# Storing the last 64 rows of each partition in two transfers of 32 rows in place of four of 16

## The chip, the cores and the metric

One core of one Trainium2 chip. The metric is the device time of one execution in microseconds (us), the median over several runs. A profiled execution also has a span, which is about 1.8 us shorter than the time and is what the views of the profile count in. DVE, ACT, POOL and SP are the chip's VectorE, ScalarE, GpSimd and SyncE; SBUF is its on-chip memory, with 128 partitions.

## The reference

A softmax over the last axis of a 16 x 1024 x 512 tensor of float32: 16,384 rows of 512, or 128 rows of 2 KB for each of the 128 partitions. 33.55 MB are read and as much is written.

```python
def reference(x):
    x_max = np.max(x, axis=-1, keepdims=True)
    exp_x = np.exp(x - x_max)
    return (exp_x / np.sum(exp_x, axis=-1, keepdims=True)).astype(np.float32)
```

## The kernel before

Data is cut into chunks of so many rows per partition, at a place (row) of one large SBUF tile of 96 rows. Chunks 8 and 9 reuse the places of chunks 0 to 3. Work goes in groups of at most 8 rows: DVE takes the row maxima, ACT the exponentials with their sums, POOL (for the last three groups DVE) multiplies by the reciprocals. SP issues the loads, ACT the stores.

```python
CHUNKS = [
    (3, 0), (5, 3), (8, 8), (16, 16), (16, 32), (16, 48), (16, 64), (16, 80), (16, 0), (16, 16),
]
...
EARLY = 8                          # loads issued at the start
AFTER_STORE = {2: [8], 3: [9]}     # these two follow the stores of chunks 2 and 3
GROUP = 8
...
STORE_ROWS = {3: 8, 4: 8, 5: 8}    # chunks 3 to 5 are stored 8 rows at a time, others whole
ON_VECTOR = 3
...
    def scale(g):
        k, a, b, since = groups[g]
        ...                        # reciprocal, then POOL or DVE multiplies
        if since is not None:
            nc.scalar.dma_start(
                out=dst[k][:, since:b, :], in_=place[k][:, since:b, :]
            )
        if b == CHUNKS[k][0]:
            for later in AFTER_STORE.get(k, ()):
                load(later)
...
        for g, (k, a, _, _) in enumerate(groups):
            ...
            rowmax(g)
            exps(g)
            if waiting is not None:
                scale(waiting)     # one group behind
            waiting = g
```

The order in the last lines matters: a store stands in ACT's program after the exponentials of the next group, and ACT waits there until the multiplication is done.

Of the kernel before, what the change touches and what calls it, by code (L numbers as in the profile page):

```python
# [1 line left out]

# [4 lines left out]

F32 = mybir.dt.float32
EXP = mybir.ActivationFunctionType.Exp
AX = mybir.AxisListType.X  # L10


CHUNKS = [
    (3, 0), (5, 3), (8, 8), (16, 16), (16, 32), (16, 48), (16, 64), (16, 80), (16, 0), (16, 16),
]
SBUF_ROWS = 96

EARLY = 8
AFTER_STORE = {2: [8], 3: [9]}

GROUP = 8

FINISH_BEFORE = (1, 2, 3)

STORE_ROWS = {3: 8, 4: 8, 5: 8}

ON_VECTOR = 3

ON_ACT = ()

AT_HEAD = {mybir.EngineType.SP: 3}



def loads_at_the_head(nc):

    main, body = nc.main_func.blocks[0], nc.main_func.blocks[1]
    for engine, count in AT_HEAD.items():
        loads = [
            i  # L40
            for i in body.instructions
            if i.engine == engine and type(i).__name__ == "InstDMACopy"
        ][:count]
        barrier = next(
            n
            for n, i in enumerate(main.instructions)
            if i.engine == engine and type(i).__name__ == "InstDrain"
        )
        for load in loads:
            body.instructions.remove(load)  # L50
        main.instructions[barrier:barrier] = loads


def one_barrier_on_exit(nc):


    end = nc.main_func.blocks[2].instructions

    def of(engine, kind):
        return [i for i in end if i.engine == engine and type(i).__name__ == kind]  # L60

    for engine in (
        mybir.EngineType.Activation,
        mybir.EngineType.PE,
        mybir.EngineType.DVE,
        mybir.EngineType.SP,
    ):
        arrivals = [i for i in of(engine, "InstDrain") if i.has_update()]
        leaves = of(engine, "InstEventSemaphore")
        assert len(arrivals) == len(leaves) == 2  # L70
        end.remove(leaves[0])
        end.remove(arrivals[1])
    gather, release, gather_2, release_2 = of(mybir.EngineType.Pool, "InstEventSemaphore")
    end.remove(release)
    end.remove(gather_2)

@with_exitstack
def kernel(
    ctx: ExitStack,
    tc: tile.TileContext,  # L80
    x: bass.AP,
    out: bass.AP,
):
    nc = tc.nc
    nc.at_finalize(loads_at_the_head)
    nc.at_finalize(one_barrier_on_exit)
    P = nc.NUM_PARTITIONS

    x_flat = x.flatten_outer_dims()
    out_flat = out.flatten_outer_dims()  # L90
    n, d = x_flat.shape
    assert n == P * sum(R for R, _ in CHUNKS)


    src, dst, at = [], [], 0
    for R, _ in CHUNKS:
        for flat, views in ((x_flat, src), (out_flat, dst)):
            part = flat[at : at + P * R, :]
            views.append(part.rearrange("(p r) d -> p r d", r=R))
        at += P * R  # L100

    data = ctx.enter_context(tc.tile_pool(name="data", bufs=1))
    stats = ctx.enter_context(tc.tile_pool(name="stats", bufs=4))
    held = data.tile([P, SBUF_ROWS, d], F32, name="held")
    place = [held[:, s : s + R, :] for R, s in CHUNKS]


    groups = []
    for k, (R, _) in enumerate(CHUNKS):
        m = -(-R // GROUP)  # L110
        cuts = [R * i // m for i in range(m + 1)]
        since = 0
        for a, b in zip(cuts, cuts[1:]):
            ends = b == R or b - since >= STORE_ROWS.get(k, R)
            groups.append((k, a, b, since if ends else None))
            since = b if ends else since
    shift = [None] * len(groups)
    sums = [None] * len(groups)

    def load(k):  # L120
        queue = nc.scalar if k in ON_ACT else nc.sync
        queue.dma_start(out=place[k], in_=src[k])

    def rowmax(g):
        k, a, b, _ = groups[g]
        shift[g] = stats.tile([P, b - a], F32, name="shift", tag="shift")
        nc.vector.reduce_max(  # L127
            out=shift[g], in_=place[k][:, a:b, :], axis=AX, negate=True
        )

    def exps(g):
        k, a, b, _ = groups[g]
        sums[g] = stats.tile([P, b - a], F32, name="sums", tag="sums")
        for r in range(a, b):
            nc.scalar.activation(  # L135
                out=place[k][:, r, :],
                in_=place[k][:, r, :],
                func=EXP,
                bias=shift[g][:, r - a : r - a + 1],
                scale=1.0,  # L140
                accum_out=sums[g][:, r - a : r - a + 1],
            )

    def scale(g):
        k, a, b, since = groups[g]
        recip = stats.tile([P, b - a], F32, name="recip", tag="recip")
        nc.vector.reciprocal(out=recip, in_=sums[g])  # L147
        on_pool = g < len(groups) - ON_VECTOR
        if on_pool:
            nc.gpsimd.tensor_tensor(  # L150
                out=place[k][:, a:b, :],
                in0=place[k][:, a:b, :],
                in1=recip.unsqueeze(2).to_broadcast([P, b - a, d]),
                op=mybir.AluOpType.mult,
            )
        for r in () if on_pool else range(a, b):
            nc.vector.tensor_scalar_mul(  # L157
                out=place[k][:, r, :],
                in0=place[k][:, r, :],
                scalar1=recip[:, r - a : r - a + 1],  # L160
# [7 lines that stand above are left out]
                load(later)  # L168

    with tc.manual_schedule():  # L170
        for k in range(EARLY):
            load(k)
        waiting = None
        for g, (k, a, _, _) in enumerate(groups):
            if waiting is not None and a == 0 and k in FINISH_BEFORE:
                scale(waiting)
                waiting = None
# [3 lines that stand above are left out]
                scale(waiting)  # L181
            waiting = g
        scale(waiting)


# [1 line left out]
_INS = ['x']  # L187
_OUTS = [((16, 1024, 512), 'float32')]


# [23 lines left out]
```

## Time and profile before

| | before |
|---|---|
| time, median of 3 | 161.61 us |
| span of the profiled run | 159.63 us |
| DVE, ACT, POOL busy | 52%, 58%, 57% |
| DMA engines | 90% or more in 37 of 40 slices |
| the four 16-row stores issued | 96.32, 110.27, 120.35, 134.00 us |
| the same stores landed | 129.93, 139.58, 149.24, 158.90 us |

How to read it: an instruction that issues a DMA takes 0.34 us in the profile, while its bytes land 25 to 34 us later. A store's turn is the landing of the store ahead of it.

### The profile page before, as it was taken

How to read it: one execution, taken by the hardware profiler on the slowest of the kernel's cores; microseconds unless marked ns; L12 is line 12 of the kernel's file. 1: busy time of each engine (PE TensorE's matmuls, PEld its weight loads, DVE VectorE, ACT ScalarE, POOL GpSimd, SP SyncE). 2: the span in 40 equal slices, each digit the busy share in tenths (PEclk: the TensorE clock that was granted, in tenths of full speed). 3: DMA queues.
4: the chain of work that ended last, by engine and by line, in shares of the span. 5: the costliest groups of instructions: out<-in, count | busy, mean ns of one | idle time of the engine just before them, and what ended most of it. 6: DMA issues, size and time to landing. Idle time of an engine off the chain costs nothing.

```text
span 159.6 us, 442 instructions
## 1 busy us (share of the span) xinstructions
DVE 82.6 (52%) x58; ACT 92.9 (58%) x257; POOL 91.2 (57%) x18
## 2 busy tenths in 40 slices
DVE  0470903980966567393856768386479935000000
ACT  0719076039949796976979957993995760000000
POOL 0060912950899999999999999999930000000000
DMA  7999999999999999999999999989999999999994
GB/s 271 439 464 398 431 391 435 458 408 421 431 423 431 427 415 443 411 468 423 431 456 411 437 423 431 464 378 448 406 468 443 445 411 419 476 411 419 468 419 172
DMA packets 3315, 67.13 MB, mean 421 GB/s; under 512 B 368, under 2 KB 368, under 8 KB 624
## 3 DMA queue, kind: packets, MB, share of 16 engines
q1 hardware_dynamic: 1440, 33.56, 49.6%
q10 hardware_dynamic: 1872, 33.56, 49.0%
q14 instruction: 3, 0.02, 0.0%
HBM read 33.55 MB, written 33.55 MB: 420 GB/s over the span
## 4 chain that ended last, share of the span: by engine, by line
POOL 51%; issue 12%; ACT 11%; DVE 7%; DMA 3%; ACTq 0%; DVEq 0%; POOLq 0%
POOL held L150 51%; ACT held L135 11%; DVE held L157 4%; DMA held<-in_x_dram 3%; DVE shift L127 3%; ACTq L163 0%; DVE recip L147 0%; DVEq L209 0%; POOLq L150 0%; DVEq L147 0%; ACTq L135 0%
## 5 line engine op out<-in xcount | busy, mean ns | idle before, releaser
L135 ACT ACTIVATE held<-held,shift 128x512 f32<-128x512 f32 x128 | 90.4, 708 | 33.0 <-POOL held L150 29.9
L150 POOL TENSOR_TENSOR held<-held,recip 128x4096 f32<-128x4096 f32 (+2 forms) x14 | 91.0, 6529 | 25.8 <-DVE recip L147 25.8
L127 DVE TENSOR_REDUCE shift<-held 128x8 f32<-128x4096 f32 (+2 forms) x17 | 70.3, 4139 | 5.4 <-DMA held<-in_x_dram 5.4
L147 DVE RECIPROCAL recip<-sums 128x8 f32<-128x8 f32 (+2 forms) x17 | 3.4, 200 | 45.9 <-ACT held L135 45.9
L135 ACT ACTIVATION_READ_ACCUMULATOR held<-held,shift 128x1 f32 x128 | 24.0, 187 | 0.0
L157 DVE TENSOR_SCALAR held<-held,recip 128x512 f32<-128x512 f32 x24 | 10.0, 491 | 0.1
L135 ACT ACT_TABLE_LOAD x1 | 1.3, 1283 | 4.5 <-DMA held<-in_x_dram 4.5
L198 POOL MEMSET const-float32-0.0<- 128x1 f32 x1 | 0.1, 98 | 0.2 <-issue 0.2
L198 POOL MEMSET const-bfloat16-1.0<- 128x1 bf16 x1 | 0.1, 101 | 0.0
L198 POOL MEMSET const-uint8-127<- 128x1 uint8 x1 | 0.1, 101 | 0.0
L198 POOL MEMSET const-float32-1.0<- 128x1 f32 x1 | 0.1, 98 | 0.0
## 6 DMA issues: line engine op xcount, KB each, us to landing
held<-in_x_dram SPq DMA_DIRECT2D x7, 4096.0 KB, 39.1
out_dram<-held ACTq DMA_DIRECT2D x4, 4096.0 KB, 29.1
out_dram<-held ACTq DMA_DIRECT2D x7, 2048.0 KB, 37.9
held<-in_x_dram SPq DMA_DIRECT2D x1, 2048.0 KB, 11.5
held<-in_x_dram SPq DMA_DIRECT2D x1, 1280.0 KB, 7.1
out_dram<-held ACTq DMA_DIRECT2D x1, 1280.0 KB, 20.5
held<-in_x_dram SPq DMA_DIRECT2D x1, 768.0 KB, 4.4
out_dram<-held ACTq DMA_DIRECT2D x1, 768.0 KB, 15.8
```

What stands on the lines that cost most here:

```text
L127: nc.vector.reduce_max(out=shift[g], in_=place[k][:, a:b, :], axis=AX, negate=True)
L135: nc.scalar.activation(out=place[k][:, r, :], in_=place[k][:, r, :], func=EXP, bias=shift[g][:, r - a : r - a + 1], scale=1.0, accum_out=s ...
L147: nc.vector.reciprocal(out=recip, in_=sums[g])
L150: nc.gpsimd.tensor_tensor(out=place[k][:, a:b, :], in0=place[k][:, a:b, :], in1=recip.unsqueeze(2).to_broadcast([P, b - a, d]), op=mybir.A ...
L157: nc.vector.tensor_scalar_mul(out=place[k][:, r, :], in0=place[k][:, r, :], scalar1=recip[:, r - a : r - a + 1],)
L198: nc = _bacc.Bacc("TRN2", target_bir_lowering=False, num_devices=1)
```

## The change

Two chunks of 32 rows replace the last four of 16. Loads are still cut at 16 rows, so that compute need not wait for more and the early places can be filled as before. Only the stores grow: 32 rows of a partition are now contiguous in DRAM, and a chunk that is not in `STORE_ROWS` is stored whole. The intent is fewer and larger transfers at the end, where only stores are left.

```diff
-CHUNKS = [
-    (3, 0), (5, 3), (8, 8), (16, 16), (16, 32), (16, 48), (16, 64), (16, 80), (16, 0), (16, 16),
-]
+CHUNKS = [(3, 0), (5, 3), (8, 8), (16, 16), (16, 32), (16, 48), (32, 64), (32, 0)]
+
+LOAD_ROWS = 16
...
-    def load(k):
-        queue = nc.scalar if k in ON_ACT else nc.sync
-        queue.dma_start(out=place[k], in_=src[k])
+    loads = [
+        (k, a, min(a + LOAD_ROWS, R))
+        for k, (R, _) in enumerate(CHUNKS)
+        for a in range(0, R, LOAD_ROWS)
+    ]
+
+    def load(i):
+        k, a, b = loads[i]
+        nc.sync.dma_start(out=place[k][:, a:b, :], in_=src[k][:, a:b, :])
...
-        for k in range(EARLY):
-            load(k)
+        for i in range(EARLY):
+            load(i)
```

More of the change, by code (lines that the diff above doesn't have):

```diff
@@ L27 @@
 ON_VECTOR = 3
-ON_ACT = ()
 AT_HEAD = {mybir.EngineType.SP: 3}
```

## The prediction

> **What bounds the kernel now.** I read the page first, then the stretches, then the order of instructions near the end, then the DMA packets. The page is misleading in one place, and that place decides this case.
>
> ```profile
> DVE 82.6 (52%) x58; ACT 92.9 (58%) x257; POOL 91.2 (57%) x18
> DMA  7999999999999999999999999989999999999994
> DMA packets 3315, 67.13 MB, mean 421 GB/s; under 512 B 368, under 2 KB 368, under 8 KB 624
> POOL 51%; issue 12%; ACT 11%; DVE 7%; DMA 3%; ACTq 0%; DVEq 0%; POOLq 0%
> ```
>
> No compute engine is over 58% busy. The DMA row is at 90% or more in 37 of the 40 slices. The chain that ended last gives POOL 51%, which looks like a bound on POOL. But its shares add up to 84%: the chain follows instructions, and its last piece is a DVE multiplication that ends at 134.0 us of 159.6. The end of the kernel is not in it. What fills the last 25.6 us is seen when the span is cut into stretches (columns: stretch and length, then busy time of DVE, ACT, POOL, the clock, the DMA share, GB/s):
>
> ```profile
> 80.00:100.00 20.00, 13.63 (x6) 16.27 (x47) 20.00 (x4) 1.00 1.00 432
> 100.00:111.00 11.00, 6.48 (x4) 8.44 (x25) 11.00 (x3) 1.00 1.01 435
> 111.00:121.00 10.00, 7.08 (x11) 10.00 (x29) 6.21 (x1) 1.00 1.01 433
> 121.00:130.60 9.60, 7.08 (x11) 6.79 (x20) 0.00 (x0) 1.00 1.01 434
> 130.60:140.30 9.70, 3.34 (x9) 0.00 (x0) 0.00 (x0) 1.00 1.01 436
> 140.30:150.00 9.70, 0.00 (x0) 0.00 (x0) 0.00 (x0) 1.00 1.00 432
> ```
>
> After 140.3 nothing computes, and the transfers run at 432 GB/s with a full DMA share, just as they did while all three engines were at work. The DMA engines have a backlog of stores to drain. The question for this change is whether the backlog ever runs dry, so I set the issues of the last stores (from the timeline) against their landings.
>
> ```profile
> 96.32 0.34 ACTq L163 DMA_DIRECT2D out_dram<-held  x1
> 110.27 0.34 ACTq L163 DMA_DIRECT2D out_dram<-held  x1
> 120.35 0.34 ACTq L163 DMA_DIRECT2D out_dram<-held  x1
> 134.00 0.34 ACTq L163 DMA_DIRECT2D out_dram<-held  x1
> ```
>
> These four are the 16-row stores, 4096 KB each. Their semaphores in the trace are full at 129.93, 139.58, 149.24 and 158.90 us from the span's start: 9.65 to 9.66 us apart, while the issues are 10 to 14 us apart. The store ahead of them (the last 8-row one) lands at 120.28. So each store is issued 10 to 34 us before its turn: issue 110.27 against a turn at 129.9 (19.7 us early), 120.35 against 139.6 (19.2), 134.00 against 149.2 (15.2). The last load packet ends at 108.16, so from there on only stores move. SP's exit wait tells the same story:
>
> ```profile
> SPq L209 <- DMA out_dram<-held: 73.9, 4, 45.1
> ```
>
> SP issues its last load at 84.50, then waits 45.1 us for the first of the four stores (to 129.9), and for the other three 9.6 us each.
>
> **What the Trainium skill says.** "DMA: Bandwidth & Descriptors", section "Where 436 GB/s comes from", puts the fabric's ceiling at 435.2 GB/s for 16 ports. The trace agrees: 4,194,304 bytes in 9.66 us are 434 GB/s, so the drain already runs at the ceiling, and larger transfers cannot make it faster. The same page, "Queues, rings and completion order", says that each DMA engine takes turns between the queues with work, a packet at a time; a queue with larger packets would then get a larger share. The loads here are done before the stores concerned come up, so no such moment exists in this trace. The same page, "Latency and other measured facts", has a table in which tiles at a row pitch of 2 MiB and more lose half their rate and at 512 KiB do not; I use it for a rival below. "Perfetto Trace Analysis", section "DMA Instruction — HWDGE (DVE, Sync)", says that the profiled window of a DMA instruction is the generation of descriptors and not the movement; the 0.34 us of a store that lands 29 us later agrees.
>
> **The change part by part.**
>
> *Compute.* A 32-row chunk is cut in four groups of 8 rows, two 16-row chunks in two and two. So there are 17 groups as before, in the same order, with the same 14 on POOL and 3 on DVE. Nothing is added or removed: 128 activations of 706 ns, 14 POOL multiplications, 24 DVE ones.
>
> *Loads.* Ten of the same sizes and in the same order, each still one run of 32 KB a partition for the last ones; the trigger for the ninth and tenth is still the stores of the third and fourth chunk, which are untouched. What moves is only where the rows lie in DRAM: partitions are 64 KB apart in place of 32 KB in the last half of the data. Cost: 0 in the first estimate.
>
> *The store at 96.32 goes.* ACT waits there for POOL: the timeline gives 2.56 us idle before the activation at 96.71. Without the store, ACT goes on at about 94.2 (its row maxima were ready at 93.1) and does its next two groups 2.5 us sooner, by about 105.6 in place of 108.1. Then it meets the store at 110.27, which waits for the POOL multiplication that ends at 110.25. POOL runs without a gap from 89.28 to 117.2 and does not move by getting its reciprocals sooner. So ACT's 2.56 us come back as a wait of about 5.1 us in place of 2.56 at 110.66. Gain: 0.
>
> *The store at 110.27 becomes the first 32-row store.* It carries what the stores of 96.32 and 110.27 carried, 8192 KB. The queue ahead of it is busy to 120.28, so it arrives 10.0 us before the DMA engines need it. Lost: 0. It will run from 120.3 to about 139.6.
>
> *The store at 120.35 goes.* That takes 0.34 us from ACT's sequencer while ACT still had queued activations. Gain on the path: 0. The DVE tail (maxima to 124.6, the last exponentials to 130.4, the last multiplications to 134.0) stays.
>
> *The store at 134.00 becomes the second 32-row store.* The first one drains to 139.6, so it is 5.6 us early. Lost: 0. It runs from 139.6 to 158.9, as the last two did.
>
> *What can be saved.* The packets' durations in the trace are 611 ns for 16 KB and 1213 ns for 32 KB on the store queue, so twice 611 less 1213 leaves 9 ns that a packet costs besides its bytes. If 64 KB a partition goes as one packet, each of the 16 DMA engines has 16 packets for these 64 rows in place of 32: 16 x 9 ns = 0.14 us. Each engine also writes two semaphore packets fewer, of 9 ns each: 0.02 us. Sum 0.16 us of 161.61, 0.1%. If software cuts 64 KB in two pieces, only the 0.02 us remain. Predicted: 161.61 - 0.16 = 161.45 us.
>
> **The rivals.**
>
> *The queue runs dry.* A store of 32 rows can't start before its last row is ready, so the usual fear with fewer and larger stores is an idle gap, and a longer tail. Were the backlog gone when the last store is issued, the kernel would end at 134.0 + 19.3 + 0.7 (the exit, 158.90 to 159.6) = 154.0 us of span, which is less than 159.6: the backlog and not the issue sets the end. This speaks clearly against it; compute would have to be late by over 5.6 us.
>
> *The freed ACT time moves the end.* If compute set the end, 2.56 us might be gained, giving 159. Against it: POOL is full there, and the drain after 134.0 is of bytes, not of instructions.
>
> *Rows are cut small.* If a run of exactly 64 KB a partition cannot be one descriptor and is cut to single rows of 2 KB, the packets' fixed part counts. From 234 ns for 6 KB and 611 ns for 16 KB, a packet costs 14 ns and 36.8 ns a KB (more than the 9 ns of the larger pair); 2 KB then takes about 87 ns, 43 ns a KB, against 37.9 for a 32 KB packet. The 38.6 us of these stores become 44.1: about +5.5 us, 167 us. It speaks against this that rows are merged to 32 KB now, and a cut in two halves would be the simple way. Chance 3%.
>
> *DRAM addresses.* With 64 KB between partitions, neighbouring DMA engines (four partitions apart, if the trace's 8 packets per engine are spread so) walk addresses 256 KB apart in place of 128 KB. The skill's table shows no loss up to 512 KiB, so I expect none; a loss of 5% on the 16-row transfers of this half would add about 3 us. Chance 2%.
>
> *Larger packets crowd out loads.* Needs loads in flight when these stores start at 120.3; the last ends at 108.2. Zero.
>
> **Range and chances.** The mechanism gives 161.45, with 0 to 0.16 us of gain. The three runs of before differ by 0.29 us, and another series of runs can sit 0.2% aside, 0.3 us. So 161.0 to 162.1 should hold 8 times in 10, with more room above because the rivals with any chance lie there. Faster by over 2% would need 3.2 us, which no DMA-bound drain at 434 GB/s has to give: 1%. Slower by over 2%: the two rivals together and some unknown, 5%. Within 2%: 94%.
>
> **What would show it right or wrong.** Right: two last stores issued near 110.3 and 134.0, landing near 139.6 and 158.8; SP's exit wait with two in place of four, the first about 55 us, the sum still about 74; ACT's wait for POOL at about 110.6 grown to about 5 us; POOL without a gap to 117; every stretch after 108 at 432 GB/s or more; packets of 64 KB near 2417 ns (twice 1213 less 9). Wrong: a stretch after 110 with a DMA share under 0.95, a last store issued after 139.6, packets of 2 KB, load packets of more than 1.25 us in the last four loads, or a start of compute that moved.

## More of the kernel before

The view of the DMA queues gives the packets: q1 is SP's queue (the loads), q10 ACT's (the stores).

```profile
q1 hardware_dynamic: 1440, 33.56, 49.6%
q10 hardware_dynamic: 1872, 33.56, 49.0%
```

## The result and the profile after

161.56 us (161.49 to 161.60, 6 runs) against 161.50 us (161.43 to 161.80, 6 runs) of the kernel before: ratio 1.0, with a 95% interval of 0.9987 to 1.0013. Same, by the 2% rule and also within a far narrower band. The small gain that was predicted cannot be seen in the times.

The queues of the changed kernel: the store queue has 288 packets fewer. 256 of them are data (512 packets of 32 KB have become 256 of 64 KB, which take 2418 ns each in the trace), 32 are semaphore writes of two transfers on 16 engines.

```profile
q1 hardware_dynamic: 1440, 33.56, 49.5%
q10 hardware_dynamic: 1584, 33.56, 48.8%
```

Most stretches of the changed kernel (columns as in the prediction: stretch, length, busy time of DVE, ACT and POOL, clock, DMA share, GB/s):

```profile
80.00:100.00 20.00, 13.75 (x7) 18.83 (x55) 20.00 (x4) 1.00 1.00 430
100.00:111.00 11.00, 6.11 (x4) 5.77 (x17) 11.00 (x3) 1.00 0.99 425
111.00:121.00 10.00, 7.35 (x11) 10.00 (x29) 6.21 (x1) 1.00 1.03 442
130.60:140.30 9.70, 3.34 (x9) 0.00 (x0) 0.00 (x0) 1.00 1.00 432
140.30:150.00 9.70, 0.00 (x0) 0.00 (x0) 0.00 (x0) 1.00 1.00 432
```

ACT has 18.83 us of work from 80 to 100 us in place of 16.27, and 5.77 in place of 8.44 in the next stretch: the removed store no longer stops it at 94 us, and it stops later instead. The DMA columns hardly move. (The page's row of 4 us slices looks ragged at the end, 312 to 574 GB/s in the ten slices before the last one. That packets of 2.4 us cross the edges of such slices is the likely reason. Over 9.70 us the rate is 432 as before.) The lines of the timeline in which ACT's wait is to be seen, with the only two stores left of the four:

```profile
110.27 0.34 ACTq L168 DMA_DIRECT2D out_dram<-held  x1
110.65 0.72 ACT L140 ACTIVATE held<-held,shift 128x512 f32<-128x512 f32 x1 [5.23 <-POOL held L155]
...
134.06 0.34 ACTq L168 DMA_DIRECT2D out_dram<-held  x1
```

In the kernel before, two waits of 2.56 us stood before the activations at 96.71 and 110.66. Here is one of 5.23. ACT's gain was handed back at the next store, which waits for the same POOL multiplication as before. A second small shift went unpredicted: DVE, also earlier, waits longer for the last load, which landed at 109.38 us in place of 109.12.

```profile
109.47 4.42 DVE L132 TENSOR_REDUCE shift<-held 128x8 f32<-128x4096 f32 x1 [3.74 <-DMA held<-in_x_dram]
```

It was 0.81 us in the kernel before, and the instruction starts 0.26 us later than there. Neither reaches the last store, issued at 134.06 against 134.00. SP's exit wait has two stores in place of four:

```profile
SPq L214 <- DMA out_dram<-held: 74.3, 2, 55.1
```

The two land at 139.58 and 158.86 us. So the end of a run can be put together from three terms, all read from semaphores and instructions in the trace: when the last 8-row store lands (from there the last 64 rows drain), how long the drain takes, and how long the exit takes after the last landing.

| us of the span | last 8-row store lands | drain | last landing | exit | span |
|---|---|---|---|---|---|
| before | 120.283 | 38.617 | 158.900 | 0.725 | 159.625 |
| after | 120.287 | 38.576 | 158.863 | 0.851 | 159.714 |

The drain did become shorter, by about 0.04 us. The exit became longer, by 0.126 us. This longer exit was not in anybody's plan, and the experiments had to say where it comes from. Both differences are smaller than the scatter of the first term: in the twelve profiles whose loads and stores have the same sizes and order up to there, the last 8-row store lands between 120.22 and 120.55 us.

### The profile page after: what moved, and what is told of

It reads as the page before. It is cut to its first block, busy times and chain, and to the rows that moved or that the text cites. A ratio compares the mean times of both kernels' runs of the same rounds, so it can differ in the third digit from the quotient of the medians.

```text
span 159.7 us, 440 instructions
## 1 busy us (share of the span) xinstructions
DVE 82.6 (52%) x58; ACT 92.8 (58%) x257; POOL 91.2 (57%) x18
## 4 chain that ended last, share of the span: by engine, by line
POOL 49%; issue 14%; ACT 11%; DVE 7%; DMA 3%; ACTq 0%; DVEq 0%; POOLq 0%
POOL held L155 49%; ACT held L140 11%; DVE held L162 4%; DMA held<-in_x_dram 3%; DVE shift L132 3%; ACTq L168 0%; DVE recip L152 0%; DVEq L214 0%; POOLq L155 0%; DVEq L152 0%; ACTq L140 0%
```

## The experiments

My theory: the store queue always has work, the drain runs at the rate of the ports, so neither the number nor the size of the last transfers sets the end. Rival A: the new places in DRAM cost what the packets gain. Rival B: the issue of the last store, or ACT's longer wait, sets the end, and gains and losses cancel there. Twelve kernels ran, and all gave correct results.

### Four stores, new places in DRAM

```diff
-STORE_ROWS = {3: 8, 4: 8, 5: 8}
+STORE_ROWS = {3: 8, 4: 8, 5: 8, 6: 16, 7: 16}     # in the changed kernel
```

> The changed kernel with its last 64 rows stored by four transfers of 16 rows again, while the rows keep their new places in DRAM (64 KB from partition to partition). My theory (the drain runs at the ports' ceiling, so neither packets nor transfers count): 161.5 us, landings 9.65 us apart, packets of 32 KB at 1213 ns. Rival A (the 64 KB pitch loses what the packets of 64 KB gain): then this one, with the pitch and without the packets, is slower than both kernels, by 0.1 to 0.3 us: 161.7.

Measured: 161.49 us, ratio 1.0 (0.9988 to 1.0013). Landings 9.65 to 9.66 us apart, packets of 1213 ns, drain 38.63 us. Against the kernel before only the addresses differ, and the drain differs by 0.01 us. Rival A falls: a cost of 64 KB from partition to partition can't be seen.

### Two transfers, old places in DRAM

```diff
+        if since is not None and k >= 6:           # in the kernel before
+            if k in (7, 9):                        # chunks 6+7 and 8+9 in one transfer each
+                ...                                # lo: the first row of the pair; s: its place
+                both = out_flat[lo : lo + 2 * rows, :].rearrange(
+                    "(c p r) d -> p c (r d)", c=2, r=16)
+                nc.scalar.dma_start(out=both,
+                    in_=held[:, s : s + 32, :].rearrange("p (c r) d -> p c (r d)", c=2))
+        elif since is not None:
```

> The kernel before with two transfers of 32 rows for its last 64 rows, each of two runs of 32 KB a partition; rows in DRAM as in the kernel before, packets of 32 KB. So the number of transfers alone. My theory: 161.5 us, the stores land at 139.6 and 158.9 us of the span. Rival A: also 161.5 or a little less. Rival B (fewer transfers lose time through ACT's longer wait or the later issue): 161.6 to 161.7, slower than the kernel before.

Measured: 161.68 us, ratio 1.0009 (0.9997 to 1.0022). Drain 38.61 us, exit 0.851 us, and the last 8-row store landed 0.13 us later than in the kernel before. By the time alone rival B's 161.6 to 161.7 was met, but the trace doesn't show its mechanism: stores issued at 110.34 and 134.14, both early, and no gap in the drain. The 0.126 us of the exit are there again, with packets of 32 KB. So the longer exit belongs to two transfers and not to packets of 64 KB. Where the 0.13 us before the drain come from is open; they lie within the scatter told above.

### Eight stores of 8 rows

```diff
-STORE_ROWS = {3: 8, 4: 8, 5: 8}
+STORE_ROWS = {k: 8 for k in range(3, 10)}         # in the kernel before
```

> The kernel before with the last 64 rows stored by eight transfers of 8 rows, packets of 16 KB at 611 ns. If a packet's fixed 9 ns of the prediction count in the drain: 512 packets more over 16 engines are 32 x 9 ns = 0.3 us, so 161.8 us; the last stores land 4.84 to 4.87 us apart. If packets overlap and the ceiling alone counts: 161.5 us and 4.83 us apart.

Measured: 161.80 us, ratio 1.0024 (1.0012 to 1.0037): slower, clear of noise (by the 2% rule still "same"), and just the 161.8 that the 9 ns gave. That the total fits is in part luck. The landings are 4.85 us apart on average, and the drain takes 38.80 us: 0.18 more than before and not 0.3. The exit, at 0.889 us, adds 0.164; the drain began 0.07 earlier. 512 packets and four transfers more cost 0.18 us, which is 5.6 ns for each of the 32 extra packets per engine: an upper bound on what one costs, as the transfers are in it.

### Packets of 2 KB

```diff
-            nc.scalar.dma_start(out=dst[k][:, since:b, :], in_=place[k][:, since:b, :])
+            for half in range(2):                  # in the changed kernel, the two last chunks
+                nc.scalar.dma_start(
+                    out=dst[k][:, since + half : b : 2, :],
+                    in_=place[k][:, since + half : b : 2, :])
```

> The changed kernel with each 32-row store replaced by two of every second row, so that no two rows are joined: packets of 2 KB for the last 64 rows, 8192 of them. The prediction's line (14 ns plus 36.8 ns a KB) gives 87 ns a packet, 512 packets per engine, 44.5 us in place of 38.6: +5.9 us, 167.4 us. If a packet's fixed part overlaps with the next packet's bytes, the drain stays near 38.6 us and the time near 161.6. In between, [...] +1.8 us, 163.3.

Measured: 171.82 us, ratio 1.0639 (1.0624 to 1.0653). A miss: slower than all three figures. The timeline of this run shows why (the second line: ACT's next activation and what it waited for):

```profile
110.38 12.56 ACTq L169 DMA_DIRECT2D out_dram<-held  x2
122.98 0.72 ACT L140 ACTIVATE held<-held,shift 128x512 f32<-128x512 f32 x1 [17.44 <-issue]
...
145.72 4.76 ACTq L169 DMA_DIRECT2D out_dram<-held  x2
```

Issuing two transfers of 2048 runs each took 12.56 us in place of 0.34 each (the second alone 11.9), and ACT could not compute meanwhile. The last stores were issued at 145.7 in place of 134.1, and the stores ahead of them had drained at 140.95. The stretch after that has a DMA share of a third:

```profile
130.60:140.30 9.70, 9.42 (x15) 7.38 (x23) 0.00 (x0) 1.00 0.98 374
140.30:150.00 9.70, 3.46 (x9) 2.14 (x7) 0.00 (x0) 1.00 0.33 124
```

### Packets of 2 KB, issued by SP

The same kernel with these stores on the other sequencer, which has nothing to do after the last load, to part the packets from the blocked ACT.

```diff
-                nc.scalar.dma_start(
+                nc.sync.dma_start(
```

> The kernel with packets of 2 KB again, its last stores issued by SP in place of ACT, as SP has nothing to do after the last load. If ACT's blocked issue (11.9 us in one store) and the dry queue after it made two thirds of the 10.3 us, and the packets themselves one third, then compute is back to 134.1 us, the queue never runs dry, and the time is 161.5 + 4 x 0.8 = 164.7 us, up to 165.5. If the packets alone made it: 171.8 again.

Measured: 165.53 us, ratio 1.0248 (1.0234 to 1.0262), at the end of what was expected (up to 165.5). The timeline merges SP's four issues into one line. Of its 33.93 us, 10.7 are a wait for the last multiplications, which the second line shows (it is one of SP's waits); the issues themselves took 0.6, 11.9, 0.5 and 9.9 us, 22.9 in all, and SP had nothing else to do:

```profile
110.23 33.93 SPq L169 DMA_DIRECT2D out_dram<-held  x4
...
SPq L169 <- DVE held L162: 10.7, 1, 10.7
```

The same two stretches as above show that the queue never ran dry:

```profile
130.60:140.30 9.70, 3.35 (x9) 0.00 (x0) 0.00 (x0) 1.00 1.04 392
140.30:150.00 9.70, 0.00 (x0) 0.00 (x0) 0.00 (x0) 1.00 1.03 383
```

So 4.0 of the 10.3 us stay when the queue never runs dry, and are put down to the packets; the other 6.3 came of the blocked ACT. (On SP the stores also take SP's own DMA queue; at its start they share the engines with the last store of ACT's.) The last two stores land 10.90 and 10.77 us after the ones ahead of them, in place of 9.66: about 12% more time for the same bytes. These packets also go to every second row, and what that alone costs was not tested.

### The last store 4.4 us later

```diff
+        if g == len(groups) - 1:                   # in the changed kernel, before the last reciprocal
+            for _ in range(1):
+                spare = stats.tile([P, b - a], F32, name="spare", tag="spare")
+                nc.vector.reduce_max(out=spare, in_=place[k][:, a:b, :], axis=AX)
```

> The changed kernel with one spare row-maximum over 8 rows (4.4 us on DVE) before the last reciprocal, so the last store is issued at about 138.5 us in place of 134.1. My theory: the first 32-row store drains to 139.6, so 1.1 us of slack are left and the time stays at 161.5. Rival (the issue of the last store sets the end): +4.4 us, 166.

Measured: 161.84 us, ratio 1.0013 (0.9992 to 1.0033), against 4.4 us of added work. The issue came at 138.19 us, the first 32-row store landed at 139.89, the second 19.30 us after it: no gap in the drain. Its span is 0.42 us longer than that of the kernel before: 0.125 are the exit, 0.02 the drain, and 0.27 lie ahead of the drain, as the last 8-row store landed at 120.55 in place of 120.28, before the spare work begins. The shift is there when the sixth load lands (51.44 us; 50.91 in the changed kernel), where the two kernels do the same work. The four runs agree to 0.1 us, so it does not come and go from run to run; what makes it is open.

### 8.8 us later, in both kernels, and 17.6 us in the kernel before

The same edit with a count of 2, then 2 and 4 in the kernel before.

> The changed kernel with two spare row-maxima, so the last store is issued at about 142.9 us, 3.3 us after the queue has run dry at 139.6. My theory: +3.3 us and up to 2 us more, since a store into an empty queue has to be set up first: 165 to 167 us. Rival: +8.8 us, 170.

> The kernel before with the same two spare row-maxima: its last store of 16 rows has 15.2 us of slack, so 8.8 us less of it leave 6.4: 161.5 us, unchanged. Rival (the issue sets the end): 170.

> The kernel before with four spare row-maxima (17.6 us), last issue at about 151.6, 2.4 us after the queue has run dry at 149.2: 164 to 166 us by my theory; 179 by the rival.

Measured: the changed kernel 166.10 us, ratio 1.0276 (1.0251 to 1.0301); the kernel before with the same 8.8 us of added work 161.47 us, ratio 0.9992 (0.9971 to 1.0012); with 17.6 us 164.89 us, ratio 1.0202 (1.0181 to 1.0223), slower, but on the edge of the 2% rule, which calls it unclear. Two stretches, first of the changed kernel and then of the kernel before, both 8.8 us late:

```profile
130.60:140.30 9.70, 9.66 (x6) 0.00 (x0) 0.00 (x0) 1.00 0.75 324
140.30:150.00 9.70, 2.35 (x6) 0.00 (x0) 0.00 (x0) 1.00 0.75 324
```

```profile
130.60:140.30 9.70, 9.66 (x6) 0.00 (x0) 0.00 (x0) 1.00 1.00 432
140.30:150.00 9.70, 2.29 (x6) 0.00 (x0) 0.00 (x0) 1.00 1.00 432
```

The kernel before again, 17.6 us late:

```profile
140.30:150.00 9.70, 9.66 (x9) 0.00 (x0) 0.00 (x0) 1.00 0.76 328
```

In the first two, the DVE column is the same but for 0.06 us. In the changed kernel the DMA share falls to 0.75 on both sides of the gap; in the kernel before it stays at 1.00. The last store was issued at 142.7 and 142.6 us; the queue ran dry at 139.65 in one and would have at 149.21 in the other. Both kernels that did run dry give the cost of starting again: the late store landed 20.75 us after its issue (19.29 of these are bytes, at the rate of the drain), in the other, the kernel before with 17.6 us, 11.09 us (9.66 are bytes). The difference is 1.46 and 1.43 us. So a store must be issued about 1.45 us before its turn if the queue is not to pause. The run before this one agrees: its lead was 1.7 us, and there was no gap. The rival's 170, 170 and 179 us are met nowhere, so the issue of the last store alone (rival B) does not set the end. This shows what the change really gives away: the slack of the last store goes from 15.2 - 1.45 = 13.8 us to 5.5 - 1.45 = 4.1 us.

### Both stores at the end

```diff
+        if since is not None and k == 6:           # in the changed kernel
+            held_back.append((dst[k], place[k]))
+        elif since is not None:
+            for o, i in held_back if k == 7 else ():
+                nc.scalar.dma_start(out=o, in_=i)
```

> The changed kernel with the first 32-row store held back until the second is ready, so that all 64 rows are issued at about 134 us. The same change taken one step on. The queue runs dry at 120.3 us and stays so until about 134.5: my theory says +14 to +16 us, 176 to 178 us. If the number of transfers or the bytes alone counted: 161.5.

Measured: 169.10 us, ratio 1.0466 (1.0451 to 1.0482). A loss by the mechanism expected, but only half as large. The stretch in which the queue was dry:

```profile
111.00:121.00 10.00, 9.96 (x11) 5.85 (x18) 6.26 (x1) 1.00 0.78 333
121.00:130.60 9.60, 7.04 (x11) 5.75 (x16) 0.00 (x0) 1.00 0.51 218
130.60:140.30 9.70, 3.43 (x9) 0.00 (x0) 0.00 (x0) 1.00 1.00 432
```

The first store went out at 126.26 us and not at 134: it waits for its own rows alone, long finished by then, and it stands in ACT's program after the last exponentials but ahead of the wait for the last multiplications. The last exponentials began at 124.72 us, and the store went out while they ran. It landed 20.78 us later, the second one 19.34 after that. 126.26 + 20.78 + 19.34 + 0.85 = 167.23, the span of this run (167.24) but for rounding.

### Loads of 32 rows

```diff
-LOAD_ROWS = 16
-EARLY = 8
-AFTER_STORE = {2: [8], 3: [9]}
+LOAD_ROWS = 32
+EARLY = 7
+AFTER_STORE = {3: [7]}
```

> The changed kernel with its two 32-row chunks also loaded by one transfer of 32 rows each (the tenth part of the change kept loads at 16 rows). The last load can only be issued when both early places are free, at about 84 us in place of 55 and 84, and compute on it starts when all 8 MB have landed. My theory: loads end at about 110 to 125 us in place of 108, the last 32 rows' compute starts up to 25 us late, the store queue runs dry after 120 to 140 us, and the time is 170 to 185 us. Rival: the backlog hides that too, 161.5 to 163 us.

Measured: 170.62 us, ratio 1.0566 (1.0549 to 1.0584). Loads ended at 110.65 us, in place of 108.33, but compute came late: DVE waited 24.0 us for loads in all (8.7 in the changed kernel), and the stores were issued at 122.88 and 146.67 us, each about 2 us after the queue had run dry. The loss is the two pauses, which compute's delay makes: of 8.6 us of span, 4.6 stand between the last 8-row store's landing and the first 32-row store's, beyond the 19.29 of its bytes, and 3.5 between the two 32-row stores'. A larger load and a larger store differ in this: a store's bytes can wait in the queue, a load's make compute wait. The first of these stores landed 21.72 us after its issue, 1 us more than the other late ones. By the times of the packets, an 8 KB packet of the instruction queue (q14, at 141.06 us) came between the data packets of one DMA engine, whose next data packet starts 0.5 us later than the others'.

```profile
DVE shift L132 <- DMA held<-in_x_dram: 24.0, 3, 12.1
ACT held L140 <- DVE shift L132: 19.6, 4, 11.3
```

### Where the exit's 0.126 us come from

The trace of SP's last instructions, before and after, without the ones that have long passed (instruction, start in us, the semaphores that it waits for; the last store's semaphore is marked):

```
before                                     after
EVENT_SEMAPHORE 158.917  S108* S101        EVENT_SEMAPHORE 158.880  S106* S100
EVENT_SEMAPHORE 158.979  S109  S102        EVENT_SEMAPHORE 158.947  S107  S99
DRAIN           159.044  S104              EVENT_SEMAPHORE 159.006  S108  S101
                                           EVENT_SEMAPHORE 159.068  S109  S102
                                           DRAIN           159.133  S104
```

SP waits for the semaphores in a fixed order, two in each instruction, about 63 ns each even where they passed long ago. Transfers take eight semaphores in turn. The 23rd transfer, the last before the change, has number 108; the 21st, the last after it, has 106, and two more instructions stand behind it. The test is a kernel with 24 transfers:

```diff
-STORE_ROWS = {3: 8, 4: 8, 5: 8}
+STORE_ROWS = {3: 8, 4: 8, 5: 8, 6: 8}             # in the changed kernel
```

> The changed kernel with its first 32-row chunk stored by four transfers of 8 rows and the second by one of 32: 24 transfers in place of 21. Theory of the exit: SP waits at the end for the transfers' semaphores in a fixed order, about 63 ns for each pair, and the last store's semaphore is the one of its turn (21 transfers: 106, two more pairs follow; 23: 108, one pair follows no more after it but one; 24: 109, the last). So from the last landing to the end of the span about 0.66 us here, against 0.85 in the changed kernel and 0.725 in the kernel before; the drain 0.09 us longer for the smaller packets; the time about 161.4 to 161.5 us. Rival (the exit is longer because a transfer of 32 rows or packets of 64 KB finish in another way): 0.85 us here too.

Measured: exit 0.662 us, with one store of 32 rows and packets of 64 KB at the end, as in the changed kernel. In all fourteen profiles the exit goes with the number of the last semaphore alone (from 106 to 103, one instruction more, by 0.03 to 0.04 us and not by 0.063):

| last store's semaphore | exit, us | kernels |
|---|---|---|
| 109 | 0.662 | last_on_late_semaphore |
| 108 | 0.723 to 0.725 | before, four stores, both "before" late, 2 KB from ACT and from SP |
| 106 | 0.850 to 0.851 | after, two stores, late by one and by two, both at the end |
| 103 | 0.882 to 0.889 | eight stores, loads of 32 |

The theory of the exit holds, and the rival (a transfer of 32 rows ends in another way) falls. The kernel itself took 161.52 us, ratio 1.0002 (0.9988 to 1.0015): drain 38.68 us, last 8-row store at 120.35. It was the one version that the experiments pointed to as perhaps better than both, and it is the same as they are. None of twelve kernels was faster than the kernel before, clear of noise.

## Why the prediction was right

- **What bounds the kernel.** Right and shown: the time did not change because a backlog of stores hid the later, larger issues. 8.8 us of added work in the kernel before changed nothing, and both kernels lost time as soon as the store queue ran dry.
- **Compute.** Right. Same groups, ACT's wait for POOL 5.23 us (about 5.1 expected), last store at 134.06.
- **Landings and SP's wait.** Right: 139.58 and 158.86 us (139.6 and 158.8 expected), a first wait of 55.1 us and a sum of 74.3. One sentence misreads its own numbers: the four stores of the kernel before were issued 15 to 24 us before their turns, not 10 to 34 (96.32 against 120.28 is the earliest, 134.00 against 149.24 the latest). From 111 us on every stretch ran at 432 GB/s or more; from 108 to 111 it was 426.
- **Loads and addresses.** Right: no cost of the 64 KB pitch (four stores in the new places). The 5% of that rival would have been 3.9 us, eight transfers of 9.66, and not 3. One of the last four loads' packets took over 1.25 us, against three before. DVE's longer wait for the last load had been missed; it is off the path.
- **What can be saved: 0.16 us.** The term that was mis-sized. Packets of 64 KB took 2418 ns, as worked out (2417), but the saving is not 9 ns a packet. Two packets on one engine overlap a little: eight of 1213 ns add up to 9.70 us, and a store of eight per engine takes 9.66. The drain lost 0.04 us in place of 0.16. The term for the exit was missing: +0.126 us. Sum: -0.04 + 0.13 = +0.09 us, the difference of the two spans (159.714 - 159.625). In the times it is less than can be told from noise, so the sign of this sum could have been anything: "same" was right because of the backlog, and these two terms had no part in it.
- **The rival of a dry queue.** Judged rightly, but the slack of 5.6 us was too large by the 1.45 us that a store needs from its issue to its turn.
- **The rival of small packets.** It did not come about; 64 KB went as one packet. Its size was wrong: 5.5 us had been worked out, 10.3 were measured when ACT issued them and 4.0 when SP did. Two errors are in it. The line through 234 ns for 6 KB and 611 ns for 16 KB has 37.7 ns a KB and 8 ns fixed, not 36.8 and 14; 2 KB then take 83 ns (85 to 86 in the traces), and the rival comes to 3.8 us, near the 4.0. And the blocked sequencer, the larger part on ACT, was not thought of.

## What to carry to other kernels

If a queue has a backlog to the end, the size of its last transfers is worth next to nothing: compare each issue with the landing of the transfer ahead of it, less the 1.45 us that a store needs here, and the difference is the slack that larger transfers use up. The change was free here because 4.1 us of 13.8 us of slack were left, and the same merge with 8.8 us more work ahead of it cost 2.8%. When two versions differ by 0.1 us, add up landing, drain and exit from the trace before explaining it: the exit order of the semaphores (0.126 us) was larger than what the change did to the drain (0.04 us), for which it was made.

## What the Trainium skill lacked or had wrong

- "DMA: Bandwidth & Descriptors", section "Where 436 GB/s comes from": the 435.2 GB/s of the ports fit, as the drain of 16,777,216 bytes in 38.58 us is 434.9 GB/s. But the section also says that between HBM and SBUF the HBM side binds, at about 358 GB/s; for this one core it did not.
- "Perfetto Trace Analysis", section "DMA Optimizations", says that larger DMA sizes saturate HBM bandwidth better, and "DMA: Bandwidth & Descriptors", section "Measured (HBM→SBUF, 128 partitions, SWDGE, issued from GpSimd)", that transfers should be 1 MiB or more. Neither says how little is left to gain above that when the queue always has work: 2 MB transfers drained 64 rows in 38.80 us, 4 MB in 38.62 and 8 MB in 38.58.
- "DMA: Bandwidth & Descriptors", section "Why small descriptors are slow (HBM only)", gives a fixed overhead of about 3 cycles for each packet. For 2 KB, 64 beats, an estimate from it is 5%; the stores of 2 KB packets took 10.17 to 10.93 us for 4 MB in place of 9.66, which is 5 to 13% (one of six was at 5%, five at 8 to 13%; left out are the one that met a dry queue and the one that ran beside the other queue's packets). They wrote every second row, so the addresses differ too; what of it is the stride was not parted.
- No page gives the time for which a sequencer is held by an issue with many runs of its data: 0.34 us for 128 runs. For 2048 runs the first of two issues took 0.5 to 0.6 us, the second 4.1 us (with the queue dry) to 11.9, on ACT and on SP.
- No page gives the lead that a large store issued by ACT needs before its turn ("DMA: Bandwidth & Descriptors" has a fixed cost for transfers that GpSimd issues, and for ACT's a time to the first byte): 1.43 to 1.49 us beyond its bytes, from issue to landing, on an empty queue, in four cases; 2.4 in a fifth, the one with the instruction packet.
- No page tells that the wait at such a kernel's end goes through the semaphores in a fixed order: about 63 ns for each instruction that follows the one of the last transfer, 0.662 to 0.889 us of exit in all.
